# Main-ring slots at multiples of 512 bytes, and feed-forward weight operands at an offset that changes from pair to pair

## The chip, the cores and the metric

The kernel runs on one core of a Trainium2 chip. The metric is the time of one execution on the device in microseconds (us); the median of several executions counts, lower is better. Engines are named as in the profile: PE is TensorE's matmul and PEld its weight load, DVE is VectorE, ACT ScalarE, POOL GpSimd, SP the engine that issues most of the DMAs.

## What is computed

One decoder layer on 512 tokens of width 2048, in 32-bit floating point:

```python
mod = silu(c) @ W_ada + b_ada          # shift1, scale1, gate1, shift2, scale2, gate2
h   = rms_norm(x) * (1 + scale1) + shift1
u   = h @ W_in                         # columns split among the groups below
y_conv = B * causal_depthwise_conv3(C * H)                 # 1024 channels
k_cmp  = compress(k, pe, w1, w2)       # blocks of 32 tokens, stride 16: gelu(flat @ w1) @ w2
y_attn = gates . (compressed, selected and sliding-window attention)   # 8 heads of 128, 2 kv heads
x = x + gate1 * (concat(rms_norm(y_conv), rms_norm(y_attn)) @ W_out)
h = rms_norm(x) * (1 + scale2) + shift2
x = x + gate2 * (relu(h @ W1) ** 2 @ W2)                   # W1: 2048 x 8192, W2: 8192 x 2048
return rms_norm(x)
```

## The kernel before

Everything lies transposed: 128 channels on the partitions, the 512 tokens along the free dimension. Each 32-bit operand is held as a high and a low part in a rounded 32-bit form (`split`, `hilo`: ACT copies the high part, DVE subtracts it from the source to get the low one), and each product is three matmuls (`mm3`): high weights by high tokens, low weights by high tokens, high weights by low tokens. A matmul's first argument is the stationary operand (128 columns, loaded by a weight load), the second streams through.

An `Order` object records every instruction and then lays out the order of issue for all engines by its own costs and due times (`plan`, `emit`), once for the projections, once for attention and once for the feed-forward part. All instructions are therefore issued from line 120, and the profile's lines carry that line; they are told apart by the names of the tiles.

The SBUF tiles that matter here:

- The main ring: 29 slots (`NMAIN`) of `SLOT` 32-bit numbers per partition, 1032 before, so 4128 bytes. Whatever is long-lived or passes between stages lies in one, as a tile with a name of its own: `x`, `h_m`, `part`, `wa` (blobs of `w_ada`), `mix`, `q`, `ct`, `chi`, `clo`, `sw`, and in the feed-forward part `tk`, the token operands. In a `tk` slot lie four blocks of 256 columns: the high and low parts of two token blocks. Since 4128 is 8 x 512 + 32, the 28 slots that `tk` uses begin at 16 different residues modulo 512 bytes, in steps of 32.
- `stage`: `raw` (three), `wh` and `wl` (two each), the weight blobs of the projections and their high and low parts, 1072 numbers wide.
- `hl`: three tiles of 2 x 1024 numbers, the high and the low part of a feed-forward weight blob; `hl_tile()` hands them out in turn. Before, all three begin at residue 64 modulo 512.

The feed-forward part multiplies by blocks of Strassen's kind, seven products per group of four weight blobs. `operands` makes the seven weight operands from four raw blobs `rw`, each into the next `hl` tile, and `run` issues 24 matmuls of 256 columns for each. A group of four blobs is a pair `p` in the first layer (`ff1(p)`, from `p = 3` to 31; the first three are done block by block, out of `plan`) and a step `q` of an eighth `f` in the second. Each has 168 matmuls. In the profile they are `pf<-tk,hl`.

`compress` makes the compressed keys and values. For each half `hf` it builds `ct`, a slot of 16 positions of 64 columns, and from it `chi` and `clo`, and then runs over 32 positions `l`, with 66 columns from column `(l % 16) * 64` of `chi` and `clo` as the stationary operand against blobs `cmp_w1` (`sw`). The last position of a half, `l % 16 == 15`, reads columns 960 to 1025, so two beyond 1024: the slot's spare columns, which a small DVE clearing (`nc.vector.memset(t[:, 1024:SLOT], 0.0)`) sets to zero. `compress` runs in the background of the convolution's projections (`w_conv`), between about 228 and 385 us.

Of the kernel before, what the change touches and what calls it, by code (L numbers as in the profile page):

```python
# [9 lines left out]
F32 = mybir.dt.float32  # L10
F32R = mybir.dt.float32r
BF16 = mybir.dt.bfloat16
AF = mybir.ActivationFunctionType
OP = mybir.AluOpType
AX = mybir.AxisListType

P = 128
T = 512
D = 2048
NK = D // P  # L20
# [3 lines left out]
NQ = T // P  # L24
# [2 lines left out]
NEG = -1e30  # L27
SCALE = HD ** -0.5
BLOB = 1072
SLOT = 1032  # L30
NMAIN = 29
NSIDE = 7
NWA = 8
NBANK = 6
SLACK = 4.0
FAST = 395e3

# [252 lines left out]
def hybrid_layer(ctx: ExitStack, tc: tile.TileContext, a, out):  # L290
    nc = tc.nc
    PSUM = bass.MemoryType.PSUM

    consts = ctx.enter_context(tc.tile_pool(name="consts", bufs=1))
# [17 lines left out]
    scr, temps = ts[0].bitcast(BF16), cycle(ts[1:])  # L312
    accums = cycle([small.tile([P, T], F32, name="sacc", tag="acc2k", bufs=2) for _ in range(2)])
    wraw = cycle([stage.tile([P, BLOB], F32, name="raw", bufs=3) for _ in range(3)])
    whl = cycle([[stage.tile([P, BLOB], F32R, name=n) for n in ("wh", "wl")] for _ in range(2)])
    accs = cycle([small.tile([P, 2], F32, name="acc") for _ in range(4)])

    def temp(shape=(P, T), dtype=F32, name=None):
# [40 lines left out]
    def mm3(ps, lh, ll, rh, rl, start, stop, more=False):  # L359
        nc.tensor.matmul(ps, lh, rh, start=start, stop=False, skip_group_check=more)  # L360
        nc.tensor.matmul(ps, lh, rl, start=False, stop=False, skip_group_check=more)
        nc.tensor.matmul(ps, ll, rh, start=False, stop=stop, skip_group_check=more)


    vec = consts.tile([P, V_END], F32, name="vec")
    order.due = 0.0
    nc.sync.dma_start(out=vec, in_=a["vec"][:, :V_END])
# [16 lines left out]


    cs = [pair(name="cs") for _ in range(2)]
    sc = small.tile([P, NK], F32, name="sc")
    nc.scalar.activation(sc, vec[:, V_C:V_ID], AF.Tanh, scale=0.5)
    nc.vector.tensor_scalar(sc, sc, 1.0, 0.5, op0=OP.add, op1=OP.mult)
    nc.vector.tensor_tensor(out=sc, in0=sc, in1=vec[:, V_C:V_ID], op=OP.mult)  # L390
# [332 lines left out]
    cw2 = pair(name="cw2").rearrange("p a b -> p (a b)")[:, :576]  # L723
    nc.sync.dma_start(out=cw2, in_=a["vec"][:, V_END:])

    def compress(which, src):
        pe = cw2[:, which * 32:which * 32 + 32]
        w2 = [cw2[:, 64 + (which * 2 + i) * P:64 + (which * 2 + i + 1) * P] for i in range(2)]
        parts = []
        for hf in range(2):  # L730
            t = slot(name="ct")
            nc.vector.memset(t[:, 1024:SLOT], 0.0)
            tv = t[:, :1024].rearrange("p (l g n) -> p l g n", g=NG, n=32)
            n = 32 - hf
            for g in range(NG):
                nc.vector.tensor_tensor(
                    out=tv[:, :, g, :n],
                    in0=src[g].rearrange("p (n l) -> p l n", l=16)[:, :, hf:],
                    in1=pe[:, hf * 16:hf * 16 + 16, None].to_broadcast([P, 16, n]), op=OP.add)
            if hf:  # L740
                nc.vector.memset(tv[:, :, :, 31:], 0.0)
            hi = slot(F32R, name="chi")
            lo = slot(F32R, name="clo")
            nc.scalar.activation(hi, t, AF.Copy)
            nc.vector.tensor_tensor(out=lo, in0=t, in1=hi.bitcast(F32), op=OP.subtract)
            parts.append((hi, lo))
            if hf:
                w = weights(a["cmp_w1"][which * 8], spare=True)
            yield
        pc = other()  # L750
        for blk in range(8):
            wh, wl = w
            hi, lo = parts[blk // 4]
            for j in range(4):
                l = blk * 4 + j
                s = slice(j * 256, (j + 1) * 256)
                m = slice((l % 16) * 64, (l % 16) * 64 + 66)
                mm3(pc[:66, :256], hi[:, m], lo[:, m], wh[:, s], wl[:, s], l == 0, l == 31)
            if blk < 7:
                w = weights(a["cmp_w1"][which * 8 + blk + 1], spare=True)  # L760
            yield
        hid = temp([P, 256], name="hid")[:64]
        tt = temp([P, 256], name="htt")[:64]
        nc.scalar.activation(hid, pc[:64, :256], AF.Copy)
        nc.vector.tensor_tensor(out=tt, in0=hid, in1=hid, op=OP.mult)
        nc.vector.tensor_scalar(tt, tt, 0.044715, 1.0, op0=OP.mult, op1=OP.add)
        nc.vector.tensor_tensor(out=tt, in0=tt, in1=hid, op=OP.mult)
        nc.scalar.activation(tt, tt, AF.Tanh, scale=math.sqrt(2.0 / math.pi))
        nc.vector.tensor_scalar(tt, tt, 1.0, 0.5, op0=OP.add, op1=OP.mult)
        nc.vector.tensor_tensor(out=hid, in0=hid, in1=tt, op=OP.mult)  # L770
        pt = other()
        for i in range(2):
            nc.tensor.transpose(pt[:, i * 64:i * 64 + 64], hid[:, i * P:(i + 1) * P], ident[:64, :64])
        hidt = temp([P, 2, NG, 32], name="hidt")
        nc.scalar.activation(hidt.rearrange("p i g n -> p (i g n)"), pt[:, :P], AF.Copy)
        yield
        if which == 0:
            pk = other()
            for i in range(2):
                nc.tensor.matmul(pk[:, :64], w2[i], hidt[:, i].rearrange("p g n -> p (g n)"),  # L780
                                 start=i == 0, stop=i == 1)
            for g in range(NG):
                split(kslc[g][:, :, :32], pk[:, g * 32:g * 32 + 32])
        else:
            pad = temp([P, 2, NG, P], name="hpad")
            nc.vector.memset(pad, 0.0)
            nc.vector.tensor_copy(pad[:, :, :, :32], hidt)
            for g in range(NG):
                pv = other()
                for i in range(2):  # L790
                    nc.tensor.matmul(pv[:, :P], pad[:, i, g], w2[i], start=i == 0, stop=i == 1)
                split(vcmp[:, g], pv[:, :P])
# [263 lines left out]
                out_conv(m)  # L1056
                m += 1

    tot = small.tile([P, NQ], F32, name="tot")
    nc.vector.tensor_tensor(out=tot, in0=ssq[:, 0], in1=ssq[:, 1], op=OP.add)  # L1060
    ra = accum("rc")
    row_bcast(lambda: next(turned), tot, 1024, ra)
# [9 lines left out]
    while m < NK:  # L1072
# [18 lines left out]
    p1s = cycle([ffp.tile([P, HT], F32, name="p1", bufs=3) for _ in range(3)])  # L1091
    sg = {t: cycle([ffp.tile([P, 1024], d, name="sg", bufs=2) for _ in range(2)])
          for t, d in (("first", F32R), ("sums", F32), ("last", F32R))}
    hl = cycle([ffp.tile([P, 2, 1024], F32R, name="hl", bufs=3) for _ in range(3)])
    banks = cycle([psf.tile([P, T], F32, name="pf") for _ in range(8)])
    LO, HI = slice(0, HT), slice(HT, T)
    halves = (LO, HI)
# [5 lines left out]
    def raw_blob(src):  # L1103
        raw = next(rw)
        nc.sync.dma_start(out=raw, in_=src)
        return raw

    def hl_tile():
        t = next(hl)
        return t[:, 0], t[:, 1]  # L1110

    def hilo(dst, src, minus=False):
        if minus:
# [267 lines left out]
    for n in range(12, 24):  # L1381
        part(n)
        if n in (17, 19, 23):
            results_of({17: 2, 19: 0, 23: 1}[n])
    for p in range(NP, 32):
        ff1(p)


# [84 lines left out]
    for f in range(8):  # L1473
        for i in range(7):
            for j in range(2):
                tok[i][j] = tslot()
                nc.sync.dma_start(out=tok[i][j].bitcast(F32), in_=gd[f][i][j].bitcast(F32))
            if f == 0 and i == T5:
                residual_pairs()
        last = f == 7  # L1480
        for q in range(3 if last else 4):
            raw = [raw_blob(a["w_f2"][4 * f + q, b]) for b in range(4)]
            ps = [{}, {}]
            for i, w in enumerate(operands(raw)):
                if f == 0 and q < 3 and i == B2:
                    residual_pairs()
                ch, first, end = CHAIN[i]
                for j in range(2):
                    mp = 2 * q + j
                    m = 2 * mp  # L1490
                    if first:
                        ps[j][ch] = bankf()
                    run(ps[j][ch], w, tok[i], first, True, 4 * j, 4)
                    b = ps[j][ch][:, :HT]
                    if i == B1:
                        if f == 0:
                            nc.scalar.activation(base[mp], b, AF.Copy)
                        else:
                            sub(base[mp], b, base[mp], OP.add)
                        if last:  # L1500
                            shared(mp)
                    elif i == U6:
                        update(m, HI, b, True)
                    elif i == T5:
                        update(m + 1, HI, b, True)
                    elif i == B2:
                        update(m, LO, b)
                        if last:
                            final(m, LO)
                    elif i == T7:  # L1510
                        update(m + 1, HI, b)
                        if last:
                            final(m + 1, HI)
                    elif i == B3:
                        update(m, HI, b)
                        if last:
                            final(m, HI)
                    else:
                        update(m + 1, LO, b)
                        if last:  # L1520
                            final(m + 1, LO)
# [92 lines left out]
```

## Time and profile before

| | |
|---|---|
| median of 3 runs | 2139.57 us (2137.35 to 2140.4) |
| profiled execution | span 2138.4 us; the page gives no time beside the span |
| projections, convolution, compress | 0 to 551 us |
| attention and output projection | 551 to 840 us |
| feed-forward, first layer | 840 to 1483 us |
| feed-forward, second layer, final norm | 1483 to 2138 us |
| HBM traffic | 211 GB/s over the span |

The span runs from the first to the last instruction of the profiled execution; the stages' bounds are read from the times of their matmuls. A row of a group reads: line, engine, operation, output<-inputs, shape, count | us in which at least one of them ran, mean ns of one | idle time of the engine just before them, and who ended it. Matmuls overlap: one is shown from its start to the modelled end of its pipeline, so its cost in a dense stretch is the distance from start to start, not its duration. A row of a window gives its bounds and length, then the busy us and count of PE, PEld, DVE, ACT and POOL, the granted TensorE clock, the DMA engines' busy share and GB/s.

### The profile page before, as it was taken

The page shows a single profiled execution, that of the slowest core. Times are in us where ns is not written, and L with a number is a line of the kernel's source. Part 1 is how long each engine was busy: PE and PEld are TensorE (multiplying, and loading weights), DVE is VectorE, ACT ScalarE, POOL GpSimd, SP SyncE. Part 2 cuts the span into 40 slices and gives each one's busy share as a digit, 9 for nine tenths or more (in the row PEclk, how much of TensorE's full clock was granted, in tenths as well). Part 3 has the DMA queues.
Part 4 walks back from the last instruction along what each step waited for, and adds up shares of the span by engine and source line. Part 5 has one row for each costly group of instructions (what it writes and reads, how often), then busy time and mean ns, then how long its engine had stood idle before and what let it go on. Part 6 is the DMA issues. An engine that isn't in the chain of part 4 may idle for free.

```text
span 2138.4 us, 37920 instructions
## 1 busy us (share of the span) xinstructions
PE 2104.6 (98%) x14978; PEld 1955.6 (91%) x14978; DVE 1900.7 (89%) x3032; ACT 1005.5 (47%) x1468; POOL 128.6 (6%) x244
## 2 busy tenths in 40 slices
PE   7999999999999999999999999999999999999998
PEld 5888787898777789999999999999999999999997
DVE  8989998888998657998999998898999999999998
ACT  4432433222555435766566566566433333333345
POOL 0000000000000001021211111111000000000000
PEclk8999999999999999999999999999999999999999
DMA  8895688877420153476666656658876366366342
GB/s 336 337 350 220 224 303 305 299 295 289 144 81 30 69 184 141 158 219 201 206 192 200 210 190 195 215 188 313 302 262 230 126 242 233 127 236 237 130 187 90
DMA packets 143106, 454.17 MB, mean 212 GB/s; under 512 B 15824, under 2 KB 18128, under 8 KB 142928
## 3 DMA queue, kind: packets, MB, share of 16 engines
q1 hardware_dynamic: 108304, 386.72, 50.0%
q0 software_dynamic: 34048, 63.98, 9.6%
q8 instruction: 118, 1.93, 0.4%
q10 hardware_dynamic: 576, 1.05, 0.1%
q14 instruction: 60, 0.49, 0.1%
HBM read 383.53 MB, written 68.16 MB: 211 GB/s over the span
## 4 chain that ended last, share of the span: by engine, by line
PE 90%; DVE 6%; DMA 1%; ACT 1%; issue 1%; SPq 0%; DVEq 0%; ACTq 0%
PE pf L120 63%; PE ps L120 22%; PE pw L120 2%; PE pv L120 1%; DVE t L120 1%; DMA wa<-in_w_ada 1%; PE s L120 1%; PE pt L120 1%; DVE nm L120 1%; DVE wl L120 1%; DVE tt L120 1%; DVE p L120 0%; DVE x L120 0%; DMA raw<-in_cmp_w 0%; DVE s L120 0%
## 5 line engine op out<-in xcount | busy, mean ns | idle before, releaser
L120 PE MATMUL pf<-tk,hl 128*128 128x256 f32 x10704 | 1264.7, 280 | 0.0
L120 PEld LDWEIGHTS pf<-tk,hl 128*128 128x128 f32 x10704 | 1263.5, 188 | 0.2 <-issue 0.2
L120 ACT ACTIVATE hl<-rw 128x1024 fp32r<-128x1024 f32 x269 | 285.1, 1060 | 356.6 <-PE pf L120 334.6
L120 DVE TENSOR_TENSOR hl<-rw,hl 128x1024 fp32r<-128x1024 f32 x269 | 328.5, 1221 | 51.2 <-ACT hl L120 50.8
L120 ACT ACTIVATE hl<-sg 128x1024 fp32r<-128x1024 f32 x180 | 191.0, 1062 | 250.6 <-PE pf L120 230.9
L120 DVE SCALAR_TENSOR_TENSOR t<-wa,cs 128x1024 bf16<-128x1024 f32 x190 | 231.7, 1220 | 16.3 <-DMA wa<-in_w_ada 15.1
L120 ACT ACTIVATE wh<-raw 128x1024 fp32r<-128x1024 f32 (+1 forms) x106 | 112.7, 1063 | 249.6 <-PE ps L120 216.7
L120 PE MATMUL ps<-h_m,wh 128*128 128x512 f32 x720 | 226.8, 394 | 0.1
L120 DVE TENSOR_TENSOR hl<-sg,hl 128x1024 fp32r<-128x1024 f32 x151 | 184.6, 1223 | 34.2 <-ACT hl L120 33.8
L120 PE MATMUL ps<-h,wh 128*128 128x512 f32 x560 | 174.4, 398 | 3.9 <-ACT h L120 3.9
L120 PEld LDWEIGHTS ps<-h_m,wh 128*128 128x128 f32 x720 | 134.7, 188 | 31.4 <-DVE h_m L120 0.6
L120 DVE TENSOR_TENSOR wl<-raw,wh 128x1024 fp32r<-128x1024 f32 (+1 forms) x106 | 129.8, 1225 | 29.1 <-ACT wh L120 25.8
L120 DVE SCALAR_TENSOR_TENSOR x<-pf,mod,x 128x256 f32<-128x256 f32 (+1 forms) x280 | 133.2, 487 | 18.0 <-PE pf L120 17.4
L120 DVE TENSOR_TENSOR sg<-sg,rw 128x1024 f32<-128x1024 f32 x120 | 146.1, 1218 | 0.0
L120 PE MATMUL ps<-h_m,wl 128*128 128x512 f32 x360 | 142.0, 394 | 0.0
L120 PEld LDWEIGHTS ps<-h,wh 128*128 128x128 f32 x560 | 105.7, 190 | 30.0 <-ACT h L120 6.3
L120 POOL DMA_DIRECT2D g<-gt x192 | 101.6, 534 | 372.9 <-issue 181.4
L120 PE MATMUL ps<-h,wl 128*128 128x512 f32 x280 | 107.7, 397 | 0.0
L120 PE MATMUL pw<-mix,wh 128*128 128x512 f32 x256 | 87.5, 404 | 0.0
L120 PEld LDWEIGHTS ps<-h_m,wl 128*128 128x128 f32 x360 | 67.6, 188 | 15.7
L120 ACT ACTIVATE t<-t 128x512 f32<-128x512 f32 (+3 forms) x131 | 74.1, 571 | 14.0 <-DVE t L120 12.1
L120 DVE TENSOR_TENSOR sg<-rw 128x1024 f32<-128x1024 f32 x60 | 73.1, 1219 | 7.2 <-DMA rw<-in_w_f 5.1
(220 smaller groups left out, 2148.4 us busy)
## 6 DMA issues: line engine op xcount, KB each, us to landing
rw<-in_w_f SPq DMA_DIRECT2D x263, 512.0 KB, 3.7
wa<-in_w_ada SPq DMA_DIRECT2D x192, 512.0 KB, 6.3
tk<-g SPq DMA_DIRECT2D x114, 512.0 KB, 6.4
g<-gt POOLq DMA_DIRECT2D x192, 256.0 KB, 3.3
raw<-in_w_conv SPq DMA_DIRECT2D x32, 512.0 KB, 5.0
x<-in_xt SPq DMA_DIRECT2D x16, 512.0 KB, 6.5
raw<-in_w_kv SPq DMA_DIRECT2D x16, 512.0 KB, 5.5
raw<-in_w_cv SPq DMA_DIRECT2D x16, 512.0 KB, 4.4
```

Source lines behind the costliest of these rows:

```text
L120: x.i, x.eng, x.call = len(self.nodes), eng, (lambda: real(*args, **kw))
```

## The change

Slots of the main ring get 1024 numbers, 4096 bytes, and a small tile `gap` ahead of them makes the ring begin at a multiple of 512, so every slot begins at residue 0 modulo 512 (and all at the same residue modulo 4096). `wh` and `wl` become 16 numbers wider, so that their residues are 384 and 128 (before 320, 0 and 192, 384); two small tiles get one buffer instead of four. The `hl` tiles become 112 numbers wider, and `hl_tile()` begins inside one at an offset such that both parts of every weight operand lie at residue 64 x `shift` modulo 512, whichever of the three tiles it is. `shift` is `p % 8` for pair `p` of the first layer and `(4 * f + q) % 8` in the second; ahead of that it is 0. The raw blobs `rw` move from residue 64 to 0.

With no spare columns in a slot, the last position of each half in `compress` reads from tiles of its own: `edge`, two of 66 columns for each half, whose last two columns are cleared once, with the other 64 copied by ACT (high part) and subtracted by DVE (low part). The four clearings of 8 columns go.

```diff
-SLOT = 1032
+SLOT = 1024
+NSHIFT = 8
-    whl = cycle([[stage.tile([P, BLOB], F32R, name=n) for n in ("wh", "wl")] for _ in range(2)])
+    whl = cycle([[stage.tile([P, BLOB + 16], F32R, name=n) for n in ("wh", "wl")] for _ in range(2)])
+    consts.tile([P, 32], F32, name="gap")
+    edges = [[attc.tile([P, 66], F32R, name=f"edge{i}{j}") for j in range(2)] for i in range(2)]
+    for e in edges:
+        for x in e:
+            nc.vector.memset(x[:, 64:].bitcast(F32), 0.0)
...
             t = slot(name="ct")
-            nc.vector.memset(t[:, 1024:SLOT], 0.0)
...
             nc.scalar.activation(hi, t, AF.Copy)
             nc.vector.tensor_tensor(out=lo, in0=t, in1=hi.bitcast(F32), op=OP.subtract)
+            last = edges[hf]
+            nc.scalar.activation(last[0][:, :64], t[:, 960:], AF.Copy)
+            nc.vector.tensor_tensor(out=last[1][:, :64], in0=t[:, 960:], in1=last[0][:, :64].bitcast(F32), op=OP.subtract)
...
-                mm3(pc[:66, :256], hi[:, m], lo[:, m], wh[:, s], wl[:, s], l == 0, l == 31)
+                ch, cl = (hi[:, m], lo[:, m]) if l % 16 < 15 else edges[blk // 4]
+                mm3(pc[:66, :256], ch, cl, wh[:, s], wl[:, s], l == 0, l == 31)
...
-    hl = cycle([ffp.tile([P, 2, 1024], F32R, name="hl", bufs=3) for _ in range(3)])
+    HLW = 2048 + 16 * (NSHIFT - 1)
+    hl = cycle([(j, ffp.tile([P, HLW], F32R, name="hl", bufs=3)) for j in range(3)])
+    shift = [0]
...
     def hl_tile():
-        t = next(hl)
-        return t[:, 0], t[:, 1]
+        j, t = next(hl)
+        lo = (16 * shift[0] - j * HLW) % (16 * NSHIFT)
+        return t[:, lo:lo + 1024], t[:, lo + 1024:lo + 2048]
...
     for p in range(NP, 32):
+        shift[0] = p % NSHIFT
         ff1(p)
...
         for q in range(3 if last else 4):
+            shift[0] = (4 * f + q) % NSHIFT
```

The order of issue in the attention and feed-forward parts stays as it was. In the projections the planner lays out the stage around `compress` differently. On ACT, where the first half's copies are made (before, then now; `wh` and `sw` are weight blobs, `y` and `vz` belong to the convolution):

```order
84 L120 ACTIVATE wh<-raw 128x1024
85 L120 ACTIVATE chi<-ct 128x1032
86 L120 ACTIVATE wh<-raw 128x1024
87 L120 ACTIVATE sacc<-y 128x512
88 L120 ACTIVATE t<-y 128x512 x2
89 L120 ACTIVATE wh<-raw 128x1024
90 L120 ACTIVATE sw<-raw 128x1024
91 L120 ACTIVATE chi<-ct 128x1032
92 L120 ACTIVATE wh<-raw 128x1024 x2
```

```order
84 L121 ACTIVATE wh<-raw 128x1024
85 L121 ACTIVATE edge_179<-ct 128x64
86 L121 ACTIVATE chi<-ct 128x1024
87 L121 ACTIVATE wh<-raw 128x1024
88 L121 ACTIVATE sacc<-y 128x512
89 L121 ACTIVATE t<-y 128x512 x2
90 L121 ACTIVATE wh<-raw 128x1024
91 L121 ACTIVATE sw<-raw 128x1024
92 L121 ACTIVATE chi<-ct 128x1024
93 L121 ACTIVATE edge_181<-ct 128x64
94 L121 ACTIVATE wh<-raw 128x1024 x2
```

One small copy stands ahead of the first half's `chi` and one behind the second's; the rest keeps its order here. On SP, where the loads of the same stage are issued (`wa` are blobs for DVE's dot products, `raw` the weight blobs), before and then now:

```order
77 L120 DMA wa<-in_w_ada 128x1024
78 L120 DMA raw<-in_cmp_w 128x1024
79 L120 DMA wa<-in_w_ada 128x1024 x3
80 L120 DMA raw<-in_cmp_w 128x1024
81 L120 DMA raw<-in_w_conv 128x1024
82 L120 DMA wa<-in_w_ada 128x1024 x2
83 L120 DMA raw<-in_cmp_w 128x1024
84 L120 DMA raw<-in_w_conv 128x1024
85 L120 DMA wa<-in_w_ada 128x1024 x3
86 L120 DMA raw<-in_cmp_w 128x1024
87 L120 DMA wa<-in_w_ada 128x1024 x2
```

```order
77 L121 DMA wa<-in_w_ada 128x1024
78 L121 DMA raw<-in_cmp_w 128x1024
79 L121 DMA wa<-in_w_ada 128x1024 x2
80 L121 DMA raw<-in_cmp_w 128x1024
81 L121 DMA raw<-in_w_conv 128x1024
82 L121 DMA wa<-in_w_ada 128x1024 x3
83 L121 DMA raw<-in_cmp_w 128x1024
84 L121 DMA raw<-in_w_conv 128x1024
85 L121 DMA wa<-in_w_ada 128x1024 x2
86 L121 DMA raw<-in_cmp_w 128x1024
87 L121 DMA wa<-in_w_ada 128x1024 x2
```

The second `cmp_w1` blob and the `w_conv` blob behind it are issued one `w_ada` blob earlier, the third pair at the same place, the fourth `cmp_w1` blob one earlier again; further on the places differ by one or two in either direction.

More of the change, by code (lines that the diff above doesn't have):

```diff
@@ L386, in hybrid_layer @@
     cs = [pair(name="cs") for _ in range(2)]
-    sc = small.tile([P, NK], F32, name="sc")
+    sc = small.tile([P, NK], F32, name="sc", bufs=1)
     nc.scalar.activation(sc, vec[:, V_C:V_ID], AF.Tanh, scale=0.5)
@@ L1057, in hybrid_layer @@
                 m += 1
-    tot = small.tile([P, NQ], F32, name="tot")
+    tot = small.tile([P, NQ], F32, name="tot", bufs=1)
     nc.vector.tensor_tensor(out=tot, in0=ssq[:, 0], in1=ssq[:, 1], op=OP.add)
```

## The prediction

> **What bounds the kernel now.** I read the busy table and the slices first, then stage windows, then groups by form, then the chain of waits inside the one stage where the order moves, and last two short stretches of the timeline.
>
> The page's first rows:
>
> ```profile
> span 2138.4 us, 37920 instructions
> PE 2104.6 (98%) x14978; PEld 1955.6 (91%) x14978; DVE 1900.7 (89%) x3032; ACT 1005.5 (47%) x1468; POOL 128.6 (6%) x244
> PE 90%; DVE 6%; DMA 1%; ACT 1%; issue 1%; SPq 0%; DVEq 0%; ACTq 0%
> ```
>
> TensorE is busy 98% of the span and holds 90% of the chain that ended last. The rest is small, so the place to look is what one matmul costs. By stage (us of window, then PE, weight load, DVE, ACT, POOL busy with counts, granted clock, DMA share, GB/s):
>
> ```profile
> 90.00:228.00 138.00, 138.00 (x596) 111.73 (x596) 127.89 (x211) 48.45 (x60) 0.00 (x0) 1.00 0.74 272
> 228.00:262.00 34.00, 33.02 (x162) 26.72 (x161) 29.70 (x47) 11.47 (x12) 0.00 (x0) 1.00 0.74 269
> 262.00:341.00 79.00, 78.61 (x389) 64.16 (x388) 70.40 (x116) 27.24 (x33) 0.00 (x0) 1.00 0.82 303
> 341.00:385.00 44.00, 42.49 (x213) 34.58 (x212) 36.03 (x61) 13.57 (x17) 0.00 (x0) 1.00 0.80 292
> 551.00:800.00 249.00, 242.56 (x1195) 189.71 (x1194) 194.60 (x476) 121.58 (x281) 1.20 (x2) 1.00 0.26 89
> 840.00:1483.00 643.00, 642.93 (x5446) 642.67 (x5446) 587.98 (x819) 406.13 (x592) 116.67 (x220) 1.00 0.63 201
> 1483.00:2119.50 636.50, 636.50 (x5395) 636.28 (x5394) 591.61 (x840) 262.40 (x298) 5.38 (x11) 1.00 0.56 204
> ```
>
> The last two rows are the feed-forward stages: 643.0 / 5446 = 118.1 ns and 636.5 / 5395 = 118.0 ns from one matmul's start to the next, clock 1.00, no idle time, DVE at 91% and 93%. DVE and ACT have room there, so this time is TensorE's own. Nearly all of it is one group:
>
> ```profile
> L120 PE MATMUL pf<-tk,hl 128*128 128x256 f32 x10704 | 1264.7, 280 | 0.0
> ```
>
> 10704 matmuls in 1264.7 us. The mean of 280 ns is the pipelined duration; the cost is 118 ns. Each streams 256 columns of a token slot `tk` while the weights of the next are loaded from `hl`. These are the two operands whose addresses the change moves. Does a matmul's cost depend on them? Two stretches of 23 matmuls of that group, same shape, same clock (start us, us, instructions):
>
> ```profile
> 1590.16 2.82 PE L120 MATMUL pf<-tk,hl 128*128 128x256 f32 x23
> ...
> 870.42 2.92 PE L120 MATMUL pf<-tk,hl 128*128 128x256 f32 x23
> ```
>
> Taking off the last one's 0.28 us, 22 steps take 2.54 and 2.64 us: 115.5 and 120.0 ns. In the first the slots read lie at 192, 256 and 384 bytes modulo 512, in the second mostly at 320, 64, 352 and 128; the weights always lie at 64. I took the start-to-start distance of all 10704 and grouped it by the slot's address modulo 512 (28 slots, 16 residues): the means go from 115.3 ns (residue 256) to 119.1 (residue 320), and a stretch on one slot repeats within about 1 ns from pair to pair. Whether DVE or ACT runs meanwhile moves the mean by under 0.7 ns. So placement matters, by a few ns, and today's 118.0 is a mean over sixteen placements.
>
> **The change part by part.**
>
> *Feed-forward.* All slots go to residue 0 and the weights to 64 times the shift, with eight shifts in turn, so the difference token minus weight takes all multiples of 64, each for one eighth of the pairs. If only that difference modulo 512 counts, the rows of before hold all eight: for 0, 64, ... 448 the means are 118.0, 117.8, 118.1, 115.3, 119.1, 118.1, 118.3 and 117.7, mean 117.8 against 118.0 over all: -0.22 ns x 10704 = -2.4 us. If the token's own residue alone counts, residue 0 has 117.7: -0.3 ns, -3 us. Both ends are near; I take -2.4. The bounds are the two stretches: all at 115.5 would be -2.5 x 10704 = -27 us, all at 120.0 +2.0 x 10704 = +21 us. Neither is likely for a mean over eight shifts: the sixteen means spread by about 1 ns (one deviation), a mean of eight by 0.35 ns, 3.8 us. What I can't see is a long run at one placement, since before no placement lasts over six matmuls; that keeps the spread wider than 3.8.
>
> On this cost the Trainium skill's page "SBUF — State Buffer", section "Who interferes with whom", says that TensorE has two independent read ports, one for the moving operand and one for the weights, and that "PE and ACT never wait on anyone". By that rule no address could matter and this term would be 0. The 115.5 and 120.0 ns above, at the same clock, don't fit it.
>
> *Front matmuls of 512 columns.* In the row 90:228 they cost 138.0 / 596 = 231.5 ns. Grouped like the others by the difference modulo 512 they go from 230.5 to 234.3; the new differences (0, 128, 256, 384) have 231.9, 232.3, 231.4 and 231.8, mean 231.85, against 232.0 for all. -0.15 ns x 2300, some of it in the attention stage where TensorE waits on others: -0.3 us.
>
> *Compress operands.* Four small ACT copies and four small DVE subtractions of 64 columns come in, four clearings of 8 columns become four of 2 at DVE's start, and the four copies and four subtractions of the whole slot lose 8 of 1032 columns. The nearest rows:
>
> ```profile
> L120 DVE TENSOR_TENSOR s<-s,cst 128x128 f32<-128x128 f32 x64 | 17.7, 291 | 1.2 <-PE s L120 1.2
> L120 ACT ACTIVATE ya<-pv 128x128 f32<-128x128 f32 x32 | 6.3, 291 | 0.0
> L120 DVE TENSOR_TENSOR clo<-ct,chi 128x1032 fp32r<-128x1032 f32 x4 | 4.9, 1224 | 0.0
> L120 ACT ACTIVATE chi<-ct 128x1032 fp32r<-128x1032 f32 x4 | 4.2, 1060 | 6.4 <-DVE ct L120 6.4
> ```
>
> At most 4 x 0.29 = 1.2 us on each engine, less 8 of 1032 columns of 1224 and 1060 ns (about 10 ns each). In 228 to 385 us DVE is busy 29.70 + 70.40 + 36.03 = 136.1 of 157 us, ACT 52.3: both hide it. Uncovered it costs at most 1.2 us on DVE, since an edge is read only by the last of each half's 16 positions. I take 0. The clearings at the start stand ahead of DVE's first work, under 0.5 us, while it waits for x: 0.
>
> *Order of issue in the same stage.* The planner, with the new instructions, lays out 228 to 385 us anew: blobs of `cmp_w1`, `w_conv` and `w_ada` change places on SP's queue, and with them DVE's dot products and TensorE's interleaving. The chain there:
>
> ```profile
> 253.84 8.20 DMA wa<-in_w_ada
> ...
> 266.23 75.61 PE ps L120 x374
> ...
> 345.39 5.81 DMA raw<-in_w_conv
> ...
> 353.65 7.47 DMA raw<-in_cmp_w
> ```
>
> It runs through three loads, yet TensorE is idle only 0.98 + 0.39 + 1.51 = 2.9 us in those windows. So a better order gains at most 2.9 us. A worse one makes a load late by one place: 512 KB at the 292 GB/s of the row 341:385 is 1.8 us, and three places, one for each load of the chain, 5.4 us. The planner's aim is the same as before; I take 0, with -2.9 and +5.4 kept for the range.
>
> The attention stage (551 to 800) keeps its order, and DVE's and ACT's instructions of 1024 columns, grouped by address, differ by under 0.6%: 0. The same goes for moving `rw` from residue 64 to 0.
>
> Sum: -2.4 - 0.3 = -2.7 us, made against the profiled execution's span of 2138.4 us. The page gives no time around the span; the median of the three runs, 2139.57, lies 1.2 us above it, and 2137.35 to 2140.4 brackets it. So 2139.6 - 2.7 = 2136.9.
>
> **The rivals.** A difference of 0.2%, 4.3 us, is about what a measurement of this kernel can tell from no change; on 10704 matmuls it is 0.4 ns each.
>
> *Long runs at good placements.* When both operands keep one difference for 168 matmuls, three of eight shifts settle at the fast stretch's 115.5: 3/8 x 2.5 = -0.94 ns, -10 us: 2129.5. For it speaks that residue 256 is fast on each of its slots (slots of that residue sit at 113.3 ns when the stretch before them was in step); against it, the means for the other seven differences lie from 117.7 to 119.1, and over all eight a slot's first three matmuls and its next three have the same mean, 117.8.
>
> *Long runs at bad placements*, the other side. With all slots equal modulo 4096 nothing breaks a bad beat between the two streams: half of the shifts settle at the slow stretch's 120.0: 4/8 x 2.0 = +1.0 ns, +10.7 us: 2150. It decides once the mean is over 118.4. For it: 120.0 is held over several steps in the row at 870.42. Against it: the differences are all in the trace and their mean is 117.8.
>
> *The planner's new order* gains its 2.9 us (2134.0) or loses 5.4 us (2142.3) on top of -2.7.
>
> *The change doesn't touch TensorE's time*: the differences seen come from something that follows the slots but isn't the address, such as the place in the pair. 2139.6, plus or minus the order's few us. Against it: in the second stage the place in the pair explains 5% of the spread, the slot's address 65%. By the rule of the Trainium skill's page "SBUF — State Buffer" named above this is the case.
>
> **How the numbers follow.** Forecast (mean near 117.8) 0.42; good runs 0.25; bad runs 0.16; new order decides 0.09 (faster 0.05, slower 0.04); untouched 0.08. Faster: 0.25 + 0.05 = 0.30. Same: 0.42 + 0.08 = 0.50. Slower: 0.16 + 0.04 = 0.20. The predicted time is the forecast's, 2136.9. Its own range, 3.8 us of placement with the order's -2.9 to +5.4, is 2131 to 2144. To leave out no more than 2 in 10 the range reaches into the good runs, to 2128, and toward the bad ones, to 2147.
>
> **What would show it.** Right: the two feed-forward stages keep 117.5 to 118.1 ns a matmul as a mean, the pairs differ with a period of eight, and the pair of shift 5 (difference 192) is the shortest: 168 matmuls at 113.4 to 115.3 are 19.1 to 19.4 us against 19.8. In 228 to 385 us TensorE idles 1 to 6 us. Wrong: the means of all pairs equal (then it isn't the difference modulo 512), or most pairs on one side of 118.0, or over 6 us of idle time around the compress matmuls.

## The result and the profile after

| | before | after |
|---|---|---|
| median | 2139.68 us (2137.35 to 2140.4, 4 runs) | 2123.97 us (2123.27 to 2124.95, 4 runs) |
| span of the profiled execution | 2138.4 us | 2123.2 us |

The ratio is 0.993, 95% interval 0.9916 to 0.9944: 15.7 us faster. The forecast was 2136.9, with a range down to 2128: the gain is about six times the one forecast, and outside the range.

First rows of the page of after (span; busy time by engine; the chain that ended last):

```profile
span 2123.2 us, 37933 instructions
PE 2088.0 (98%) x14978; PEld 1941.9 (91%) x14978; DVE 1897.1 (89%) x3036; ACT 1006.0 (47%) x1472; POOL 128.2 (6%) x244
PE 87%; DVE 9%; DMA 2%; issue 1%; ACT 1%; SPq 0%; DVEq 0%; ACTq 0%
```

The same 14978 matmuls keep TensorE busy for 2088.0 us where it was 2104.6. The bound is the same; one matmul costs less. The windows of after, in the columns shown before, and the feed-forward group:

```profile
90.00:228.00 138.00, 138.00 (x597) 111.83 (x596) 127.89 (x212) 47.90 (x59) 0.00 (x0) 1.00 0.74 273
228.00:262.00 34.00, 33.64 (x164) 27.38 (x163) 30.04 (x48) 12.99 (x16) 0.00 (x0) 1.00 0.74 263
262.00:341.00 79.00, 77.92 (x385) 63.37 (x384) 69.84 (x115) 26.77 (x34) 0.00 (x0) 1.00 0.84 301
341.00:385.00 44.00, 44.00 (x221) 36.23 (x220) 38.19 (x63) 14.99 (x18) 0.00 (x0) 1.00 0.86 313
840.00:1477.00 637.00, 637.00 (x5454) 636.80 (x5454) 585.99 (x817) 404.81 (x587) 115.74 (x219) 1.00 0.65 204
1477.00:2104.50 627.50, 626.50 (x5364) 626.04 (x5364) 587.56 (x837) 260.40 (x296) 5.26 (x10) 1.00 0.58 205
```

```profile
L121 PE MATMUL pf<-tk,hl 128*128 128x256 f32 x10704 | 1251.4, 280 | 1.0 <-DVE x L121 0.5
```

The feed-forward stages: 637.0 / 5454 and 626.5 / 5364 = 116.8 ns from matmul to matmul, against 118.1 and 118.0, at the same clock of 1.00. Matched matmul by matmul, the first layer takes 7.0 us less and the second 5.3 less, 12.2 of the 15.2 us between the spans. The other 3 us lie ahead of them: the matmuls of 512 columns cost 231.1 ns on average instead of 232.2. In 228 to 385 us TensorE idles 0.36 + 1.08 + 0 = 1.4 us (2.9 before).

One statement made above about the code was wrong. The three `hl` tiles don't lie in SBUF in the order in which they are used: the second lies in the third place. The formula in `hl_tile()` assumes the order of use, so only the first tile's operands lie at 64 x `shift`; the others lie 64 below and 64 above it. The difference between token and weight address therefore changes with every weight operand, every 24 matmuls, and not from pair to pair. The lengths of the pairs repeat after 12 pairs (four differences modulo 256 by three tiles), to 0.01 us but for one pair with two waits in it, and not after eight.

Grouped by the difference of the moving operand's address minus that of the weights, the 24 matmuls of an operand cost in after (pairs of differences that are 256 apart agree within 0.2 ns, so it is taken modulo 256; "from" is the operand before; the last column averages the prediction's eight means in pairs):

| difference | after, mean | by what came before | before, mean |
|---|---|---|---|
| 0 | 119.8 ns | 120.0 whatever came before | 118.6 |
| 64 | 113.8 ns | from 0: 113.4 in 71 of 72; from a quick 192: quick in 26 of 26; from a slow 192: slow in 5 of 5; from 128 (two operands alone): about 118 | 118.0 |
| 128 | 118.4 ns | three at 115.8, then 119 | 118.2 |
| 192 | 115.0 ns | from a quick 64: 113.6; from 128: quick in 40 of 67, else about 118 | 116.5 |

Differences 64 and 192 have two levels, a quick one near 113.4 ns and a slow one near 117.7, and what came before goes with the one or the other. For 192 entered from 128 one has to look two operands back: with 0 ahead of the 128 it was slow in 25 of 25, with 64 there quick in 35 of 37. These are the "two states" of the expectations below.

### The profile page after: what moved, and what is told of

It is laid out like the page before. It is cut to its first block, busy times and chain, and to the rows that moved or that the text cites. A ratio compares the mean times of both kernels' runs of the same rounds, so it can differ in the third digit from the quotient of the medians.

```text
span 2123.2 us, 37933 instructions
## 1 busy us (share of the span) xinstructions
PE 2088.0 (98%) x14978; PEld 1941.9 (91%) x14978; DVE 1897.1 (89%) x3036; ACT 1006.0 (47%) x1472; POOL 128.2 (6%) x244
## 3 DMA queue, kind: packets, MB, share of 16 engines
q10 hardware_dynamic: 576, 1.05, 0.1%
## 4 chain that ended last, share of the span: by engine, by line
PE 87%; DVE 9%; DMA 2%; issue 1%; ACT 1%; SPq 0%; DVEq 0%; ACTq 0%
PE pf L121 61%; PE ps L121 21%; PE pw L121 2%; DVE t L121 1%; PE pv L121 1%; DVE wl L121 1%; DVE nm L121 1%; DMA rw<-in_w_f 1%; DVE x L121 1%; DMA wa<-in_w_ada 1%; PE pt L121 1%; DVE tt L121 1%; DVE hl L121 1%; PE s L121 1%; DVE p L121 1%
## 5 line engine op out<-in xcount | busy, mean ns | idle before, releaser
L121 PE MATMUL pf<-tk,hl 128*128 128x256 f32 x10704 | 1251.4, 280 | 1.0 <-DVE x L121 0.5
L121 PEld LDWEIGHTS pf<-tk,hl 128*128 128x128 f32 x10704 | 1250.0, 189 | 1.4 <-issue 0.7
L121 DVE SCALAR_TENSOR_TENSOR t<-wa,cs 128x1024 bf16<-128x1024 f32 x190 | 232.0, 1221 | 9.7 <-DMA wa<-in_w_ada 8.3
```

Source lines behind the costliest of these rows:

```text
L121: x.i, x.eng, x.call = len(self.nodes), eng, (lambda: real(*args, **kw))
```

## The experiments

The theories: **A**, the difference modulo 256 alone sets the cost; **B**, slots at multiples of 512 as such; **C**, an offset that keeps changing; **D**, the new order of issue; **E**, a difference has two levels, set by what the stream meets on entry and ended by a stall; **F**, difference 64 settles at 117.6 ns in any long run. A was my first reading of the table's means.

### One difference throughout

Every weight operand of the feed-forward part at difference 64, or at 0:

```diff
-    HLW = 2048 + 16 * (NSHIFT - 1)
+    HLW = 2048 + 64
-        lo = (16 * shift[0] - j * HLW) % (16 * NSHIFT)
+        lo = 16 * shift[0]              # shift[0] stays 3, or 0
```

> The changed kernel with one placement throughout: every feed-forward weight operand at residue 192 modulo 256, the token slots at 0, so that token minus weight is 64 modulo 256 for all 10704 matmuls. Theory A (the difference modulo 256 sets the cost of a matmul, as the changed kernel's trace has it: 0 119.9 ns, 64 113.7, 128 118.4, 192 114.9): 10704 x (113.7 - 116.7) = -32 us, about 2092 us. Theory B (slots at multiples of 512 are what helps, whatever the weights' offset): 2124 us, as the changed kernel. Theory C (changing the offset all the time is what helps): slower than the changed kernel, about 2139 us.

Measured: 2133.2 us, ratio 0.9962 [0.9939, 0.9986]; eight of nine executions from 2131.5 to 2135.4, one at 2112.17. That one has no profile; it lies about 21 us below the others, which is what 4,800 matmuls at 113.4 ns in place of 117.7 would save, so that it may have kept the quick level through one layer is an inference.

> The same with the difference 0 throughout. Theory A: 10704 x (119.9 - 116.7) = +34 us against the changed kernel, about 2158 us, slower than before the change though its slots lie at multiples of 512. Theory B: 2124 us. Theory C: about 2139 us.

Measured: 2159.24 us, ratio 1.0097 [1.0082, 1.0112]. Stretches of 520 us in the dense feed-forward, of the kernel with difference 0:

```profile
950.00:1470.00 520.00, 520.00 (x4335) 520.00 (x4335) 470.89 (x624) 314.07 (x442) 96.88 (x184) 1.00 0.63 196
1550.00:2070.00 520.00, 520.00 (x4335) 520.00 (x4335) 477.87 (x655) 193.00 (x184) 2.64 (x5) 1.00 0.57 203
```

520 / 4335 = 120.0 ns, as A said. The kernel with difference 64, two windows of 55 us and one of 520:

```profile
855.00:910.00 55.00, 55.00 (x485) 55.00 (x484) 53.12 (x94) 39.75 (x69) 7.44 (x14) 1.00 0.57 177
925.00:980.00 55.00, 55.00 (x469) 55.00 (x468) 51.63 (x70) 35.01 (x49) 10.18 (x20) 1.00 0.70 215
950.00:1470.00 520.00, 520.00 (x4418) 520.00 (x4417) 474.52 (x636) 323.47 (x452) 97.39 (x184) 1.00 0.64 202
```

55 / 485 = 113.4 ns, then 55 / 469 = 117.3 and 520 / 4418 = 117.7: same addresses, same clock, two levels. Between them, in the timeline:

```profile
916.25 2.86 PE L121 MATMUL pf<-tk,hl 128*128 128x256 f32 x22 [0.49 <-DVE hl L121]
...
919.74 1.54 PE L121 MATMUL pf<-tk,hl 128*128 128x256 f32 x11 [0.63 <-DVE t L121]
```

TensorE idles 0.49 and 0.63 us for DVE, and the stream does not get back to the quick level in the next 10,000 matmuls. So A falls, and E and F were formed.

### The parts alone

The edges and the new order of issue, with the slots and the feed-forward weights placed to each other as before:

```diff
-SLOT = 1024
+SLOT = 1032
-        lo = (16 * shift[0] - j * HLW) % (16 * NSHIFT)
-        return t[:, lo:lo + 1024], t[:, lo + 1024:lo + 2048]
+        return t[:, 0], t[:, 1]         # and no gap, wh and wl as before
```

> The kernel before with the compress part of the change alone: tiles of their own for the last position and the planner's new order, all placements as before. Theory A: only the 1.3 us that the stage from matmul 880 to 1650 gained in the changed kernel's trace, about 2138 us. Theory D (the order makes the gain): 2124 to 2128 us.

Measured: 2139.23 us, ratio 1.0002 [0.9993, 1.0011]. All engines work through the instructions in the changed kernel's order here, so that order is worth nothing; D falls.

The kernel before with weight offsets that change from pair to pair, slots still 4128 bytes:

```diff
+        shift[0] = p % NSHIFT           # NSHIFT = 4; (4 * f + q) % NSHIFT in the second layer
-        return t[:, 0], t[:, 1]
+        lo = (16 * shift[0] - (0, 2, 1)[j] * HLW) % (16 * NSHIFT)
+        return t[:, lo:lo + 1024], t[:, lo + 1024:lo + 2048]
```

> The kernel before, slots of 4128 bytes, with weight operands whose residue modulo 256 changes from pair to pair (0, 64, 128, 192). The difference then changes with the slot, every six matmuls, and is an odd multiple of 32 for half of them. Theory A, with the step that a placement has to last for its cost to show: the mean stays at 118 ns, 2138 to 2140 us. Theory C: about 2124 us. If a placement need not last, and odd multiples of 32 cost the same as their neighbours, the mean would be the changed kernel's 116.7 ns and the time 2125 us.

Measured: 2139.32 us, ratio 1.0003 [0.9994, 1.0012]; 118.0 ns. An offset that keeps changing brings nothing while the slots differ: C falls in this form. Neither half of the change brings the 16 us by itself: the slots with one fixed difference gave 2133.2 and 2159.2, the changing offsets alone nothing.

### The same four differences in another order

The changed kernel with the formula mended, so that all operands of a pair share one difference (168 matmuls) and the order of differences is 0, 192, 128, 64:

```diff
-        lo = (16 * shift[0] - j * HLW) % (16 * NSHIFT)
+        lo = (16 * shift[0] - (0, 2, 1)[j] * HLW) % (16 * NSHIFT)
```

> The changed kernel with the offset made to follow the pair as meant: all seven weight operands of a pair have one residue, so the difference modulo 256 stays for 168 matmuls and goes 0, 192, 128, 64, 0, ... from pair to pair (in the changed kernel it changes with each operand of 24, since the three weight tiles don't lie in the order in which they are used). Theory A (the difference alone sets the cost): 10704 matmuls by their differences, 3000 x 119.9 + 2520 x 113.7 + 2664 x 118.4 + 2520 x 114.9 ns, +2 us against the changed kernel, 2126 us. Theory E (differences 64 and 192 have two steady states, 113.5 and 117.6 to 118 ns, and the difference before and stalls decide which; 64 is fast after 0 and slow after 128): 64 is now always entered from 128 and costs 117.6; 192 after 0 was never seen: 2133 us if it lands fast, 2144 us if slow.

Measured: 2143.22 us, ratio 1.0021 [1.0011, 1.003]: 19 us slower than the changed kernel, with the same slots, the same four differences and nearly the same share of each. By the trace 192 after 0 and 64 after 128 stay at 117.8 ns for all 168 matmuls, in every pair. The first pair, the only one at 64 that is entered from 0, has 113.4 ns. A (2126 by the shares) and B can't make this difference; it is the slower of E's two forecasts.

### Entering on purpose

One operand (24 matmuls) in every second pair at difference 0, all others at 64; and the same with 128 in place of 0:

```diff
-        lo = (16 * shift[0] - j * HLW) % (16 * NSHIFT)
+        lo, shift[0] = 16 * shift[0], 3
-        shift[0] = p % NSHIFT
+        shift[0] = 0 if p % 2 else 3    # 2 in place of 0 for the other kernel; q % 2 in the second layer
```

> Difference 64 throughout, but the first weight operand of every second pair at difference 0 (720 matmuls of 10704). Theory E: each such operand puts what follows back into the fast state, which holds till the next stall: 9984 x 113.5 + 720 x 120 ns, about -30 us against the changed kernel, some 3 us given back after stalls: 2097 us. Theory A is the same within 2 us (2097), but it had failed on difference 64 throughout (2133 measured, 2092 expected). Theory F (difference 64 settles at 117.6 ns in any long run): 2134 us.

Measured: 2101.48 us (2100.77 to 2102.15), ratio 0.9821 [0.9805, 0.9838].

> The same with the operand at difference 128 in place of 0: as many changes of the offset, from the other side. Theory E: 64 entered from 128 lands slow: 9984 x 117.6 + 720 x 118.4 ns, +10 us against the changed kernel, 2134 us. Theory C (any change of the offset helps): as with 0, about 2097 us.

Measured: 2134.5 us, ratio 0.9978 [0.9968, 0.9987]. The two kernels differ in the address of one weight operand in fourteen. With 0, two pieces of the timeline (a reset, and a stretch behind it) and the window:

```profile
948.58 3.27 PE L121 MATMUL pf<-tk,hl 128*128 128x256 f32 x26
...
954.74 3.34 PE L121 MATMUL pf<-tk,hl 128*128 128x256 f32 x28
```

```profile
950.00:1470.00 520.00, 520.00 (x4572) 520.00 (x4570) 488.53 (x657) 332.96 (x466) 100.23 (x190) 1.00 0.69 215
```

and the window with 128:

```profile
950.00:1470.00 520.00, 520.00 (x4414) 520.00 (x4413) 473.37 (x632) 323.58 (x452) 97.09 (x184) 1.00 0.65 202
```

The first row is nearly all reset: taking off the last one's 0.28 us, 25 steps in 2.99 us, 120 ns. The second has 27 steps in 3.06 us, 113.4 ns. Over 520 us that is 113.7 ns with 0 and 117.8 ns with 128: 24 dear matmuls make the next 312 cheap. E's 2097 was 4.5 us low: it allowed for stretches behind stalls that stay slow until the next reset, but not for TensorE waiting more, 9.8 us ahead of the `tk` matmuls in place of the changed kernel's 6.4. F's 2134 is out.

### Finer steps

Differences in steps of 16 bytes, 168 matmuls each, and the same for `wh` and `wl` in the front:

```diff
-NSHIFT = 8
+NSHIFT = 16
-        lo = (16 * shift[0] - j * HLW) % (16 * NSHIFT)
+        lo = (4 * shift[0] - j * HLW) % (4 * NSHIFT)
+        at = 4 * (blobs[0] % 16) if cols == 1024 and not spare else 0   # blobs[0] += 1 for each blob
+        wh, wl = wh[:, at:at + cols], wl[:, at:at + cols]
```

> A map, one look: the difference modulo 256 goes down by 16 bytes from pair to pair (168 matmuls at each), and the weight blobs of the projections step by 16 bytes from blob to blob (matmuls of 512 columns). Theory E: 0 at 120.0, 128 at 118.4; 64, entered from 80, either 113.5 or 117.6. No theory has numbers for the differences between; if all offsets of 16 in between cost about 118 the odd multiples of 32 of the kernel before were no cause by themselves. Projections: 227.9 ns at difference 0 and 232.9 at 128, as in the changed kernel.

Measured, one execution: 2142.12 us. Entered from the difference 16 above, the means from 0 upward were 120.0, 119.9, 116.7, 116.7, 117.8, 118.1, 120.0, 118.7, 118.7, 120.0, 118.7, 118.8, 114.5, 117.9, 118.4 and 118.3 ns. Only 192 reached the quick level, in three stretches of four. For 512 columns 0, 16, 64 and 80 cost 227 to 230 ns, the others 231 to 234. Entered in this way, none of the differences between the multiples of 64 is under 116.7 ns.

### Whose address it is

The changed kernel with all ring slots 64 bytes further on, and with them all that lies behind them, the weight operands too. Every operand keeps its difference, and both of its addresses change:

```diff
-    consts.tile([P, 32], F32, name="gap")
+    consts.tile([P, 48], F32, name="gap")
```

> The changed kernel with all main-ring slots 64 bytes further on (at 64 over a multiple of 256), the weight operands turning as in it. Two states by the difference (E): the same cycle of differences, so the same time, about 2124 us, and the costs of the feed-forward matmuls move with the difference: weights at 64 over a multiple of 256 (difference 0) now 120.0 ns, weights at a multiple of 256 (difference 64) now 113.4 to 115. If the weights' own address decides: weights at a multiple of 256 stay at 119.9, those at 64 over stay at 114.8. If the slots have to lie at multiples of 512 (B): all differences become alike, about 118 ns, and 2137 us.

Measured, one execution: 2126.36 us. By the weights' own address modulo 256 (0, 64, 128, 192) the means were 119.8, 115.0, 118.4 and 113.8 ns in the changed kernel and are 113.8, 119.8, 115.0 and 118.4 here. Each operand kept its cost while its address moved by 64, so neither the weights' nor the slots' own address sets it; what stayed is the difference. B falls with it, since no slot lies at a multiple of 512 here.

### The front, and how long the quick level lasts

The kernel with resets, with the front's `wh`, `wl` and `h` tiles 128 bytes further on, so that the `h_m` matmuls get difference 0 in place of 128:

```diff
+    stage.tile([P, 32], F32, name="gap2", bufs=1)
     whl = cycle([[stage.tile([P, BLOB + 16], F32R, name=n) for n in ("wh", "wl")] for _ in range(2)])
```

> The kernel with a reset in every second pair, and the weight tiles and token tiles of the front stages moved by 128 bytes, so that the 1,080 matmuls of 512 columns on the h_m tiles have difference 0 in place of 128. Two states by the difference (E): those go from 232.9 to 228 ns, the same as the h tiles have at difference 0, so 5 us less than 2101.5, about 2096. If the cost there comes from the h_m slots themselves or the state of the front is set otherwise: 2101.5, and 232.9 ns stays. The feed-forward stays at 113.7 ns for difference 64 by both.

Measured: 2097.29 us (2096.12 to 2098.46), ratio 0.9803 [0.9789, 0.9818]. The `h_m` instructions alone (PE, weight load, DVE, ACT busy with counts), of the kernel with resets and then of this one:

```profile
90.00:228.00 138.00, 107.16 (x460) 85.84 (x459) 5.53 (x8) 5.02 (x8) 1.00 0.74 273
```

```profile
90.00:228.00 138.00, 107.21 (x472) 88.10 (x470) 5.51 (x8) 5.02 (x8) 1.00 0.74 274
```

107.16 / 460 = 233.0 ns became 107.21 / 472 = 227.1 ns. About 1070 such matmuls make 6.3 us, of which 4.2 arrived. The rest is lost ahead of the feed-forward part: its first matmul starts at 838.6 us in place of 841.9, 3.3 us earlier, since TensorE idles 26.6 us before it where it was 23.5.

The kernel with resets, but only in four pairs, behind the stalls near 920 and 1520 us:

```diff
-        shift[0] = 0 if p % 2 else 3
+        shift[0] = 0 if p in (4, 5) else 3
-            shift[0] = 0 if q % 2 else 3
+            shift[0] = 0 if 4 * f + q in (3, 4) else 3
```

> As the kernel with a reset in every second pair (difference 0 for one operand, 24 matmuls, else 64), but with the resets in four pairs alone: pairs 4 and 5 of the first half, pairs 3 and 4 of the second, just after the stalls. Two states that only a stall or a bad neighbour ends (E): the fast state, 113.5 ns, then lasts for over 4,000 matmuls in each half, 650 matmuls at 120 fall away: 2095 to 2097 us. If a long run at 64 settles at 117.6 by itself (F; the fast stretch of the kernel with difference 64 throughout was 506 matmuls): about 2130 us, with fast stretches of a few hundred matmuls after each reset.

Measured: 2096.47 us (2094.91 to 2097.93), ratio 0.9801 [0.9785, 0.9817].

```profile
950.00:1470.00 520.00, 520.00 (x4590) 520.00 (x4589) 489.08 (x659) 333.47 (x467) 100.56 (x190) 1.00 0.70 218
1550.00:2070.00 520.00, 518.75 (x4573) 518.47 (x4571) 498.67 (x719) 219.36 (x244) 0.00 (x0) 1.00 0.54 190
```

520 / 4590 = 113.3 ns; the quick level held for 4,823 matmuls behind one reset. F falls: it doesn't wear off.

Both edits together:

> The two last edits together: the front tiles moved by 128 bytes, and resets in four pairs alone. Two states by the difference (E): the stages don't touch each other, so both gains add: 2101.5 - 4.2 - 5.0 = 2092 us, with the h_m matmuls at 227 ns and the feed-forward at 113.4 ns for thousands of matmuls on end. If the fast state was found by luck of the stalls in the kernel with rare resets: anything from 2092 to 2105, with a slow stretch at 117.6 ns that goes from a stall to the next reset or to the end of the layer.

Measured: 2108.65 us median of six, ratio 0.9824 [0.979, 0.9858], but in two groups: 2090.1 and 2091.23, and four from 2108.38 to 2112.35. The profile is of one of the four:

```profile
950.00:1470.00 520.00, 520.00 (x4591) 520.00 (x4590) 488.41 (x658) 332.00 (x463) 99.69 (x189) 1.00 0.71 219
1550.00:2070.00 520.00, 520.00 (x4415) 519.83 (x4415) 488.32 (x681) 203.62 (x205) 0.00 (x0) 1.00 0.54 189
```

The first layer is at 113.3 ns, the second at 117.8. The timeline where the level goes, 6 us behind the last reset:

```profile
1542.59 4.92 PE L121 MATMUL pf<-tk,hl 128*128 128x256 f32 x42
...
1546.21 1.22 DVE L121 TENSOR_TENSOR hl<-rw,hl 128x1024 fp32r<-128x1024 f32 x1
...
1547.71 2.64 PE L121 MATMUL pf<-tk,hl 128*128 128x256 f32 x21
...
1550.54 1.59 PEld L121 LDWEIGHTS pf<-tk,hl 128*128 128x128 f32 x13 [0.17 <-DVE hl L121]
```

41 steps in 4.64 us, 113.2 ns, and then 20 in 2.36, 118.0. Between these two rows of PE stands one step of 131 ns, at 1547.58 us, 18 ns more than its neighbours; no idle time is shown for it. It is the second matmul of a new operand, whose weight load starts at 1547.48, just after DVE ends an `hl` tile at 1547.43; that the load waited for it is likely, not shown. The wait of 0.17 us for DVE's `hl` comes 3 us later, when the level is gone. The remaining 4,500 matmuls pay 4.4 ns each, 20 us. That is the distance between the two groups; the two quick executions themselves have no profile, so that they kept the level is an inference from their time. E's 2092 is right for two of six; the rival's upper end of 2105 was too low. E is also incomplete: a wait that makes a step of 1.05 us, at 1507 us in this profile, turned the slow level into the quick one with no difference 0 in between, so a wait can leave either level behind it. The version to use is the one with a reset in every second pair and the front moved: 2097 us, within 2.4 us in four executions, since a lost level comes back within two pairs.

## Why the prediction was wrong

**Right:** what bounds the kernel (TensorE, 98%), that placement moves a matmul's cost, the edges at 0 and the order of issue at 0 (the kernel with these alone: 1.0002), and 1 to 6 us of idle time around `compress` (1.4).

**Wrong: the feed-forward term.** It was put at -2.4 us and measured -12.2 (the matmuls' means give -1.27 ns x 10704 = -13.6; two steps of 0.76 and 0.80 us in the second layer take 1.3 back). The step that failed is "for 0, 64, ... 448 the means are ... mean 117.8": it took the means over stays of six matmuls as the price of a difference. They are averages over two levels and over what the stream met before. Difference 64 had 118.0 there and has 113.8 where it is mostly entered from 0: a quarter of the matmuls at 4.2 ns less, 1.05 of the 1.27 ns. The text had the clue in hand ("slots of that residue sit at 113.3 ns when the stretch before them was in step") and used it as a remark, not as a second variable.

**The spread** of 3.8 us came from the same step: sixteen means, taken as independent draws. The two extremes, 115.5 and 120.0, were taken as bounds, but the quick level is 113.4.

**The description** of the change had the difference last for a pair. Had it been so, the time would have been 2143.2 (the kernel with the mended formula), slower than before the change: the gain itself is luck, made by a tile order that was not the one meant. The period of eight pairs, and the pair of shift 5 as the shortest, were wrong for the same reason.

**512 columns:** -0.3 predicted. The mean fell by 1.05 ns x some 2540 = -2.7 us, most of it on the `h` tiles, 231.7 to 227.9 ns at difference 0, while `h_m` at 128 rose from 232.0 to 233.0.

**The rivals.** Long runs at good placements (2129.5) was the nearest in kind and still 5.5 us short, since it sized the quick level by a mixed stretch. Long runs at bad placements is also real: difference 0 throughout gave 2159.2. "Untouched" is refuted: the kernels with 0 and with 128 as the reset issue the same instructions and differ by 33 us. The rule of the Trainium skill's page "SBUF — State Buffer", section "Who interferes with whom", by which TensorE's two read ports are independent and it never waits on another, doesn't fit if, as in the prediction, no address can matter by it: 113.4, 117.7 and 120.0 ns stand here for one shape at clock 1.00.

## What to carry to other kernels

When a dense stream of matmuls shows several costs for one shape, group them by the difference between the moving and the weight address and also by what came just before; a mean over short stays says little on long ones. Read from the built program where each tile lies; the order in which tiles are made or used doesn't give it, as the three `hl` tiles show. Compare a whole stretch by count per window (4335, 4418 and 4590 in 520 us here) before reading single rows. A gain that depends on a level that a short wait can end has to be re-entered regularly; a version that sets it once can be the fastest in one execution and 20 us slower in the next.

## What the runs showed of the hardware that was not expected

- The same matmul of 256 columns, with its weight load, costs 113.4, 117.7 or 120.0 ns by the difference of its two addresses modulo 256 and by history. At difference 64 both 113.4 and 117.7 last for thousands of matmuls.
- 24 matmuls at difference 0 led to the quick level in 71 of 72 cases in the changed kernel; 24 at 128 led to the slow one at 64 in all 30 cases of the kernel that has them. Very little ended the quick level: a step of 131 ns in the last kernel and one of 148 ns, near 1500 us, in the kernel with a reset in every second pair, where 113 is usual. But near 920 us a step of 0.48 us ended it in that kernel, and one of 0.49 us in the kernel with rare resets did not. Which waits end it or bring it back, and what in the chip holds the level, is open.
- After the idle time of 2.1 us in the kernel with the front moved, the granted clock of the next window was 0.66, with 28 matmuls in 5 us where the window ahead has 56 in 6:

```profile
1500.00:1506.00 6.00, 6.00 (x56) 6.00 (x55) 3.77 (x6) 2.78 (x4) 0.53 (x1) 1.00 1.04 406
1506.00:1509.00 3.00, 1.05 (x10) 0.85 (x8) 2.25 (x2) 1.06 (x1) 0.00 (x0) 1.00 1.00 386
1509.00:1514.00 5.00, 4.83 (x28) 4.83 (x29) 5.00 (x9) 0.95 (x1) 0.00 (x0) 0.66 0.67 224
```

  A wait of this length doesn't always do so: behind a step of 2.43 us near 2068 us, the kernel with rare resets keeps its clock:

```profile
2070.90:2075.00 4.10, 4.10 (x35) 4.05 (x35) 2.98 (x7) 1.35 (x4) 0.00 (x0) 1.00 0.00 0
```

- At the quick level DVE is busy 498.67 of 520 us in the second layer, 96%. It is close to being the next bound, and the idle times of TensorE shown above, which go with a lost level, are for DVE.
